# Attention heads whose small matrix products are set side by side on TensorE, in a streaming-encoder block

## The chip, the cores and the metric

One core of one Trainium2 chip runs the whole program. The metric is the device time of one execution in microseconds (us), as the median of several runs. TensorE (PE in the profile; PEld is its weight load), VectorE (DVE), ScalarE (ACT), GpSimd (POOL) and the queue of SyncE (SP) that issues most transfers each run their own list of instructions in order, and wait for each other through semaphores.

## What is computed

One layer over 256 tokens of width 4096, all in float32. A normalized input `xn` is projected to seven parts; 16 attention heads of width 128 and a convolution module run beside each other; their gated outputs are projected back, and a second gated embedding follows.

```python
xn = rms_norm(h, norm_in_g[i])
q, k, v, z_a, a_c, g_c, z_c = split(xn @ w_in[i])           # 4 x 2048, 3 x 2048 columns
y_a = chunked_attention(q, k, v, rel_table[i])              # softmax(q k / sqrt(128) + bias) v
y_a = rms_norm(y_a, attn_out_g[i]) * silu(z_a)
y_c = conv_module(a_c, g_c, w_dw[i], ...)                   # u = a * sigmoid(g); 31 taps; LayerNorm; swish; @ w_pw
y_c = rms_norm(y_c, conv_out_g[i]) * silu(z_c)
h = h + concatenate([y_a, y_c]) @ w_out[i]
h = h + sigmoid(rms_norm(h, g) @ w_ple_gate[i] + b) * (p[i] @ w_ple[i])
return rms_norm(h, final_g)
```

With 256 tokens every query block of 128 rows sees only the keys before it: the first block 128 keys, the second 256. So a head's scores are one 128x128 and one 128x256 product, and its probabilities are three blocks of 128x128.

## The kernel before, in words

**The large products.** Every float32 operand of a large product is split into a high part and a remainder (`wh` and `wl` for weights, L199 to L210), and each product is made of three matmuls, high by high, low by high, high by low, at L420. Here these are called **wide steps**: one matmul that moves 512 columns into a PSUM bank. `mixed_product` (L377) walks the weights two row blocks at a time. A weight block arrives in `wt` (five buffers) by a transfer on SP's queue (L480, L482); ScalarE casts it to `wh` and VectorE subtracts to give `wl` (L204, L205; three buffers each); then TensorE takes 12 wide steps on it. Some pairs of blocks ("sevens") use seven products in place of eight, with helper sums `ua` and `uh`, `ul`, and their helper banks are taken from the same four small PSUM banks (`tmp_ps`, L86) that attention uses.

**The small products.** All of these are plain float32 matmuls into `tmp_ps`, and they are called **narrow passes** here: a transpose is one pass of 128 columns, any other float32 product is two passes for each matmul, which the profile shows as two records. They are:

- the transposes of the gated convolution input in `glu_conv` (L822), eight in each of four calls;
- the transposes of queries and keys in `to_heads` (L943);
- for each head in `attention` (L953): the scores S (L958, L959); after the softmax the three transposes T of the probabilities `s` (L977); ScalarE's copy of them to `pT` (L979); the three weighted sums W over the values (L982 to L984).

**Softmax between S and T.** VectorE scales the scores and adds the bias (L965), takes the negative row maximum (L969); ScalarE takes the exponent with the row sums (L970); VectorE takes the reciprocal (L974). After W, ScalarE scales the result into `y` (L986), which lies over the head's own queries.

**What sets the order.** The code is written stage after stage (L1042 to L1063): `glu_conv`, projections of queries, keys and values, `attention(g)` for one group of four heads, and so on for four groups, called group 0 to 3 here. A scheduler of the framework then merges the stages: it goes through the program with priorities by the order in which it is written, places each instruction on its engine when it expects the inputs to be there, and fills the gaps with wide steps of the next stage. That merged order is fixed when the program is built; on the chip each engine only follows its list. So a head's narrow passes stand scattered among the wide steps of the product that comes next in the code. Work put into the list `later` (the taps of the convolution, L787; the LayerNorm of the convolution, L862 to L913) is handed out between the wide steps too. The LayerNorm's centering (L868), squares (L872) and sums (L876) follow right behind group 2.

Of the kernel before, what the change touches and what calls it, by code (L numbers as in the profile page):

```python
# [16 lines left out]
P = 128  # L17
# [8 lines left out]
def hybrid_block(  # L26
# [23 lines left out]
    nc = tc.nc  # L50
    _, T, D = x.shape
    NH = T // P
# [3 lines left out]
    HD = AW // H  # L56
# [5 lines left out]
    GH = NB // HD  # L62
# [23 lines left out]
    def tmp_psum():  # L86
        return ps_tmp.tile([P, 512], F32, tag="tmp", name="tmp_ps")
# [41 lines left out]
    ident = cpool.tile([P, P], F32, name="ident")  # L129
# [210 lines left out]
    def units(text):  # L340

        return [
            (int(u.rstrip("*+-")), "".join(f for f in "*+" if f in u), "-" in u)
            for u in text.split()
        ]
# [4 lines left out]
    first = units("0 1 3 5 7 9 11 13 15 2* 8 4* 10 6* 12 14")  # L350
# [236 lines left out]
    def scaled_pair(w, col, apart, order, r, fills, homes=(), **kw):  # L587

        t, z = [], []

        def on_helpers(helper):
            for dst, src in zip((t, z), sum_tiles(*homes)):
                dst.extend(src)
            nc.scalar.activation(z[0][0], helper["P1"], AF.Identity, scale=r[:, :1])
            helper_sums(helper, z)
            for h, j in QUARTERS[1:]:
                nc.scalar.activation(z[h][j], z[h][j], AF.Identity, scale=r[:, h : h + 1])

        c = mixed_product(w, col, xT, xS, order, on_helpers, fills=fills, apart=apart, **kw)
        for h, j in QUARTERS:  # L600
            stt(
                z[h][j], c[h][j], r[:, h : h + 1], z[h][j],
                ALU.mult, ALU.subtract if j else ALU.add,
            )
        return t

    def square_sum(dst, src, scale=1.0):
        junk = spool.tile([P, NB], mybir.dt.bfloat16, tag="junk", name="junk", bufs=1)
        to = junk.rearrange("q (g d) -> q g d", d=src.shape[2]) if len(src.shape) == 3 else junk[:, : src.shape[1]]
        return nc.scalar.activation(to, src, AF.Square, scale=scale, accum_out=dst)  # L610
# [191 lines left out]
    def glu_conv(c):  # L802
        if c == 0:
            sg, gate = scaled_pair(
                w_in0, o_a, o_g - o_a, first, r_x, (1,), begin=first_pairs
            )
        else:
            sg, gate = scaled_pair(
                w_in0, o_a + c * NB, o_g - o_a,
                *((early, r_x, early_fills) if c == 1 else (early_seven, r_x, seven_fills)),  # L810
                ahead=more_combinations if c == 2 else None,
            )
        for h in range(NH):
            nc.scalar.activation(gate[:, h, :], gate[:, h, :], AF.Sigmoid)
            tt(sg[:, h, :], sg[:, h, :], gate[:, h, :], ALU.mult)
        uT = spool.tile([P, 4, T], F32, tag="hd", name="uT", bufs=5)
        for pair in range(2):
            pt = tmp_psum()
            for i in range(2):
                for h in range(NH):  # L820
                    b = 2 * pair + i
                    nc.tensor.transpose(  # L822
                        pt[:, i * T + h * P : i * T + (h + 1) * P],
                        sg[:, h, b * P : (b + 1) * P],
                        ident,
                    )
            nc.scalar.copy(
                uT[:, 2 * pair : 2 * pair + 2, :], pt.rearrange("q (i t) -> q i t", t=T)
            )
        cv = act.tile([P, 4, T], F32, tag="act", name="cv")  # L830
        for i in range(4):
            for k in reversed(range(TAPS)):
                later.append(partial(conv_tap, cv, uT, i, 4 * c + i, k))
        conv.append(cv)
# [118 lines left out]
    def attention(g):  # L953
        qT, kT, v, bias = qs[g], ks.pop(g), vs.pop(g), biases.pop(g)
        y = qT.rearrange("q g (h d) -> q h g d", h=NH)
        for hd in range(GH):
            sp = tmp_psum()
            nc.tensor.matmul(sp[:, :P], qT[:, hd, :P], kT[:, hd, :P], start=True, stop=True)  # L958
            nc.tensor.matmul(sp[:, P : P + T], qT[:, hd, P:], kT[:, hd, :], start=True, stop=True)  # L959
            s = spool.tile([P, P + T], F32, tag="s", name="s")  # L960
            nm = spool.tile([P, NH], F32, tag="nm", name="nm")
            den = spool.tile([P, NH], F32, tag="den", name="den")
            for h, (lo, hi) in enumerate(((0, P), (P, P + T))):
                n = hi - lo
                nc.vector.scalar_tensor_tensor(  # L965
                    s[:, lo:hi], sp[:, lo:hi], HD ** -0.5, bias[:, hd, n - 1 :: -1],
                    ALU.mult, ALU.add,
                )
                nc.vector.tensor_reduce(nm[:, h : h + 1], s[:, lo:hi], AX.X, ALU.max, negate=True)  # L969
                nc.scalar.activation(  # L970
                    s[:, lo:hi], s[:, lo:hi], AF.Exp, bias=nm[:, h : h + 1],
                    accum_out=den[:, h : h + 1],
                )
            nc.vector.reciprocal(den, den)  # L974
            pt = tmp_psum()
            for j in range(3):
                nc.tensor.transpose(pt[:, j * P : (j + 1) * P], s[:, j * P : (j + 1) * P], ident)  # L977
            pT = spool.tile([P, 3 * P], F32, tag="pT", name="pT")
            nc.scalar.copy(pT, pt[:, : 3 * P])  # L979
            o = tmp_psum()  # L980
            vc = slice(hd * HD, (hd + 1) * HD)
            nc.tensor.matmul(o[:, :HD], pT[:, :P], v[:, 0, vc], start=True, stop=True)  # L982
            nc.tensor.matmul(o[:, HD : 2 * HD], pT[:, P : 2 * P], v[:, 0, vc], start=True, stop=False)
            nc.tensor.matmul(o[:, HD : 2 * HD], pT[:, 2 * P :], v[:, 1, vc], start=False, stop=True)  # L984
            for h in range(NH):
                nc.scalar.activation(  # L986
                    y[:, h, hd], o[:, h * HD : (h + 1) * HD], AF.Identity, scale=den[:, h : h + 1]
                )
        for h in range(NH):
            square_sum(ssq_a[:, h, g : g + 1], y[:, h])  # L990
        y_a.append(y)
# [48 lines left out]
    n_g = H // GH  # L1040
    assert n_g == CW // NB == 4
    glu_conv(0)  # L1042
    glu_conv(1)
    load_bias(0)
    heads((o_q, 0), (o_k, 0))
    heads((o_v, 0), (o_v, 1))
    attention(0)
    glu_conv(2)
    load_bias(1)
    heads((o_q, 1), (o_k, 1))  # L1050
    attention(1)
    glu_conv(3)
    moved = comb_place(spool, "hd", bufs=5)
# [3 lines left out]
    heads((o_q, 2), (o_k, 2))  # L1057
    heads((o_q, 3), (o_v, 2), order=early_six, fills=six_fills)
    attention(2)
    layer_norm_swish()  # L1060
    load_bias(3)
# [105 lines left out]
    for ys, o_z, r_y in ((y_a, o_za, r_a), (y_c, o_zc, r_c)):  # L1167
        for c0 in range(0, len(ys), 2):
            last = ys is y_c and c0 + 2 == len(ys)
# [9 lines left out]
    pT = []  # L1179
# [160 lines left out]
    def sum_of(h, at):  # L1340
        s = end[:, 0, h : h + 1]
        pin(nc.vector.tensor_reduce(s, ssq_f[:, h, :at], AX.X, ALU.add))
        return s
# [36 lines left out]
    for i, cols in enumerate(halves):  # L1380
        part = ps_acc.tile([P, NB], F32, tag="acc", name="part")
# [7 lines left out]
    s = sum_of(1, n_f + 1)  # L1389
# [35 lines left out]
```

## Time and profile before

| what | value |
|---|---|
| median of three runs | 2025.72 us (2024.74 to 2026.13) |
| the profiled execution's own time | 2025.85 us |
| span of its instructions | 2024.1 us |
| PE busy | 2006.7 us (99%) |
| DVE busy | 1926.9 us (95%) |
| ACT busy | 1257.1 us (62%) |
| mean granted TensorE clock | 0.998 |
| the four attention groups begin at | 356.6, 536.6, 797.7 and 893.8 us |

The profiled execution took 1.75 us longer than its span; that part lies before the first and behind the last instruction. Matmuls overlap in the records (a wide step lasts 391 ns on average and the next begins about 227 ns after it), so a step's price is the distance to the next one and not its own length. The chain of waits gives just these distances: it walks back from the end, and each piece is the time by which its instructions pushed the chain on. "x8" after a piece is the number of matmuls in it.

### The profile page before, as it was taken

The page shows a single profiled execution, that of the slowest core. Times are in us where ns is not written, and L with a number is a line of the kernel's source. Part 1 is how long each engine was busy: PE and PEld are TensorE (multiplying, and loading weights), DVE is VectorE, ACT ScalarE, POOL GpSimd, SP SyncE. Part 2 cuts the span into 40 slices and gives each one's busy share as a digit, 9 for nine tenths or more (in the row PEclk, how much of TensorE's full clock was granted, in tenths as well). Part 3 has the DMA queues.
Part 4 walks back from the last instruction along what each step waited for, and adds up shares of the span by engine and source line. Part 5 has one row for each costly group of instructions (what it writes and reads, how often), then busy time and mean ns, then how long its engine had stood idle before and what let it go on. Part 6 is the DMA issues. An engine that isn't in the chain of part 4 may idle for free.

```text
span 2024.1 us, 26329 instructions
## 1 busy us (share of the span) xinstructions
PE 2006.7 (99%) x9043; PEld 1648.0 (81%) x9043; DVE 1926.9 (95%) x2771; ACT 1257.1 (62%) x1634; POOL 65.3 (3%) x71
## 2 busy tenths in 40 slices
PE   9999999999999999999999999999999999999997
PEld 7888888878888888788888888887888888888876
DVE  7999999899999999888999999999999999999998
ACT  7655555665666556776566676765766766656565
POOL 0000000000000000000000000000000000000000
PEclk9999999999999999999999999999999999999999
DMA  8788878679668877556677786876767766666765
GB/s 290 225 233 241 249 221 250 178 220 257 200 198 257 255 206 235 164 176 205 202 239 215 225 244 209 240 239 204 236 215 230 234 200 200 211 218 206 232 207 180
DMA packets 174193, 447.72 MB, mean 221 GB/s; under 512 B 14302, under 2 KB 17518, under 8 KB 174058
## 3 DMA queue, kind: packets, MB, share of 16 engines
q1 hardware_dynamic: 161952, 417.93, 63.8%
q0 software_dynamic: 11456, 27.27, 7.9%
q8 instruction: 71, 1.16, 0.2%
q10 hardware_dynamic: 650, 0.84, 0.1%
q14 instruction: 64, 0.52, 0.1%
HBM read 441.78 MB, written 4.19 MB: 220 GB/s over the span
## 4 chain that ended last, share of the span: by engine, by line
PE 89%; DVE 6%; issue 2%; DMA 1%; ACT 1%; POOLq 0%; POOL 0%; ACTq 0%; DVEq 0%; SPq 0%
PE acc L420 68%; PE acc_P L420 17%; DVE wl L205 2%; DMA wt<-in_w_in_dram 1%; PE tmp_ps L170 1%; DVE cv L787 1%; PE acc L237 1%; DVE ul L205 1%; PE tmp_ps L959 0%; PE tmp_ps L943 0%; PE tmp_ps L977 0%; ACT uh L204 0%; DVE cv L868 0%; ACT wh L204 0%; PE tmp_ps L982 0%
## 5 line engine op out<-in xcount | busy, mean ns | idle before, releaser
L420 PE MATMUL acc<-wh,big_t 128*128 128x512 f32 x4028 | 1240.3, 391 | 0.9 <-ACT big_t L156 0.4
L204 ACT CAST wh<-wt 128x1024 fp32r<-128x1024 f32 (+1 forms) x716 | 684.3, 965 | 493.8 <-PE acc L420 351.7
L420 PEld LDWEIGHTS acc<-wh,big_t 128*128 128x128 f32 x4028 | 753.3, 188 | 157.1 <-issue 1.3
L205 DVE TENSOR_TENSOR wl<-wt,wh 128x1024 fp32r<-128x1024 f32 (+1 forms) x716 | 788.8, 1113 | 33.0 <-ACT wh L204 27.5
L420 PE MATMUL acc<-wl,big_t 128*128 128x512 f32 x1958 | 756.4, 392 | 0.3 <-DVE wl L205 0.2
L420 PEld LDWEIGHTS acc<-wl,big_t 128*128 128x128 f32 x1958 | 367.2, 188 | 78.1 <-DVE wl L205 2.7
L204 ACT CAST uh<-ua 128x1024 fp32r<-128x1024 f32 x187 | 196.6, 1051 | 103.0 <-DVE ua L519 51.7
L205 DVE TENSOR_TENSOR ul<-ua,uh 128x1024 fp32r<-128x1024 f32 x187 | 228.1, 1220 | 6.9 <-ACT uh L204 4.2
L787 DVE SCALAR_TENSOR_TENSOR cv<-uT,dw,cv 128x255 f32<-128x255 f32 (+23 forms) x480 | 203.6, 463 | 1.1
L420 PE MATMUL acc_P<-uh,big_t 128*128 128x512 f32 x570 | 174.6, 391 | 0.1
L204 ACT CAST uh<-ub 128x1024 fp32r<-128x1024 f32 x99 | 104.2, 1053 | 47.9 <-DVE ub L532 39.2
L420 PEld LDWEIGHTS acc_P<-uh,big_t 128*128 128x128 f32 x570 | 106.0, 188 | 24.5 <-ACT uh L204 3.3
L205 DVE TENSOR_TENSOR ul<-ub,uh 128x1024 fp32r<-128x1024 f32 x99 | 120.8, 1220 | 0.8 <-ACT uh L204 0.5
L420 PE MATMUL acc_P<-ul,big_t 128*128 128x512 f32 x285 | 109.7, 392 | 0.2 <-DVE ul L205 0.2
L420 PE MATMUL acc<-uh,big_t 128*128 128x512 f32 x286 | 88.6, 390 | 0.0
L420 PE MATMUL acc_P<-wh,big_t 128*128 128x512 f32 x286 | 88.3, 389 | 0.0
L518 DVE TENSOR_TENSOR ua<-wt 128x512 f32<-128x512 f32 x112 | 76.9, 686 | 10.0 <-DMA wt<-in_w_in_dram 6.2
L519 DVE TENSOR_TENSOR ua<-wt 128x512 f32<-128x512 f32 x112 | 76.8, 686 | 2.7 <-DMA wt<-in_w_in_dram 1.7
L420 PE MATMUL acc_P<-uh,comb_t 128*128 128x512 f32 x228 | 70.3, 391 | 0.3 <-ACT uh L204 0.2
L532 DVE TENSOR_TENSOR ub<-ub,wt 128x512 f32<-128x512 f32 x99 | 68.1, 688 | 1.4
L531 DVE TENSOR_TENSOR ub<-ua,wt 128x512 f32<-128x512 f32 x99 | 67.8, 685 | 0.0
L420 PEld LDWEIGHTS acc_P<-ul,big_t 128*128 128x128 f32 x285 | 53.3, 188 | 13.9 <-DVE ul L205 3.0
(254 smaller groups left out, 1631.0 us busy)
## 6 DMA issues: line engine op xcount, KB each, us to landing
wt<-in_w_in_dram SPq DMA_DIRECT2D x416, 512.0 KB, 4.7
wt<-in_w_out_dram SPq DMA_DIRECT2D x128, 512.0 KB, 4.5
wt<-in_w_ple_gate_dram SPq DMA_DIRECT2D x128, 512.0 KB, 4.2
wt<-in_w_pw_dram SPq DMA_DIRECT2D x32, 512.0 KB, 4.9
ua<-in_w_in_dram SPq DMA_DIRECT2D x31, 512.0 KB, 4.3
ua<-in_w_in_dram POOLq DMA_DIRECT2D x31, 512.0 KB, 8.8
wt<-in_w_in_dram SPq DMA_DIRECT2D x31, 256.0 KB, 2.8
low<-in_w_in_dram POOLq DMA_DIRECT2D x12, 512.0 KB, 8.2
```

The lines of the kernel that those rows point to most:

```text
L170: nc.tensor.transpose(pt[:, i * T + h * P : i * T + (h + 1) * P], src[:, h, b] if len(src.shape) == 4 else src[:, h, b * P : (b + 1) * P], ...
L204: nc.scalar.copy(wh[:, :kc, :], wt[:, :kc, :]),
L205: nc.vector.tensor_tensor(wl[:, :kc, :], wt[:, :kc, :], wh[:, :kc, :].bitcast(F32), ALU.subtract),
L237: nc.tensor.matmul(acc, a, b[:, k, :], start=kb == 0 and kind == 0, stop=kb == kblocks - 1 and kind == 2,)
L420: nc.tensor.matmul(banks[name], a, b, start=name not in begun, stop=final and ends[name] == n and kind == 2 and not (left and name in "P2 ...
L518: plus(ua[:, 0], w0[:, 0], w0[:, 1])
L519: plus(ua[:, 1], w0[:, 1], w1[:, 1])
L531: plus(ub[:, 0], ua[:, 0], w1[:, 1])
L532: plus(ub[:, 1], ub[:, 0], w1[:, 0])
L787: nc.vector.scalar_tensor_tensor(cv[:, i, PAD - k :], uT[:, i, : T + k - PAD], dw[:, b, k : k + 1], cv[:, i, PAD - k :], ALU.mult, ALU.add,)
```

## The change

Attention is cut into three functions: `scores` (S and the softmax), `turned` (T and its copy) and `weighted` (W and the scaling). They are called in a new order: T of a head, W of the head before it, S of the head after it. A helper, `tensor`, ties each of these matmuls to the one before by a dependency without a semaphore, which binds only the scheduler: the chain keeps T, W, S in that order on TensorE, and since all inputs of W and S are there before those of T, nothing stands between them. The three transposes are taken in the order 1, 2, 0. In `glu_conv` the transposes go through the halves of the tokens in reverse (the later half first).

```diff
@@ glu_conv
         for pair in range(2):
             pt = tmp_psum()
-            for i in range(2):
-                for h in range(NH):
+            for h in reversed(range(NH)):
+                for i in range(2):
                     b = 2 * pair + i
                     nc.tensor.transpose(
@@ attention
         y = qT.rearrange("q g (h d) -> q h g d", h=NH)
-        for hd in range(GH):
+        behind = []
+
+        def tensor(ins):
+
+            if behind:
+                tc.add_manual_dep(
+                    ins.ins, behind[0].ins.name,
+                    mybir.DependencyInfo(mybir.DependencyClass.NoSync, mybir.DependencyReason.DATA),
+                    reason="a head's matrix work in one run",
+                )
+            behind[:] = [ins]
+
+        def scores(hd):
+
             sp = tmp_psum()
...
             nc.vector.reciprocal(den, den)
+            return s, den
+
+        def turned(s):
+
             pt = tmp_psum()
-            for j in range(3):
-                nc.tensor.transpose(pt[:, j * P : (j + 1) * P], s[:, j * P : (j + 1) * P], ident)
+            for j in (1, 2, 0):
+                tensor(
+                    nc.tensor.transpose(pt[:, j * P : (j + 1) * P], s[:, j * P : (j + 1) * P], ident)
+                )
             pT = spool.tile([P, 3 * P], F32, tag="pT", name="pT")
             nc.scalar.copy(pT, pt[:, : 3 * P])
+            return pT
+
+        def weighted(hd, pT, den):
+
...
+        ready, old = scores(0), None
+        for hd in range(GH):
+            s, den = ready
+            pT = turned(s)
+            if old:
+                weighted(*old)
+            old = hd, pT, den
+            if hd + 1 < GH:
+                ready = scores(hd + 1)
+        weighted(*old)
```

In the rows below, `s` are a head's probabilities, `pT` their transposes, `z` the values, `qT` and `kT` queries and keys, and `acc_...` the banks of the large product that runs meanwhile. In the changed program L971 and L973 are S, L997 is T and L1011 is W.

On TensorE, in group 2, this stood around the third head before the change:

```order
L420 MATMUL acc_7214<-wl,big_t 128x512
L977 MATMUL tmp_ps<-ident,s 128x128
L420 MATMUL acc_7213<-wh,big_t 128x512 x2
L977 MATMUL tmp_ps<-ident,s 128x128 x2
L420 MATMUL acc_7213<-wl,big_t 128x512
L420 MATMUL acc_7215<-wh,big_t 128x512 x2
L982 MATMUL tmp_ps<-z,pT 128x128
L983 MATMUL tmp_ps<-z,pT 128x128
L984 MATMUL tmp_ps<-z,pT 128x128
L958 MATMUL tmp_ps<-kT,qT 128x128
L959 MATMUL tmp_ps<-kT,qT 128x256
L420 MATMUL acc_7215<-wl,big_t 128x512
```

And this stands there now:

```order
L420 MATMUL acc_7213<-wh,big_t 128x512 x2
L420 MATMUL acc_7213<-wl,big_t 128x512
L997 MATMUL tmp_ps<-ident,s 128x128 x3
L1011 MATMUL tmp_ps<-z,pT 128x128 x3
L971 MATMUL tmp_ps<-kT,qT 128x128
L973 MATMUL tmp_ps<-kT,qT 128x256
L420 MATMUL acc_7215<-wh,big_t 128x512 x2
```

A head had three separate places among the wide steps (one transpose, two transposes, then its weighted sums with the next scores); now it has one, and the weighted sums in it are those of the head before. Over the four groups there were 52 places with narrow passes and there are 21 now. Between S and the first T stood 8, 7 and 7 wide steps for the later heads of this group, and 16, 12 and 12 stand there now.

At the end of group 2, TensorE has the last head's transposes and sums and then the LayerNorm's mean (L856). Before:

```order
L977 MATMUL tmp_ps<-ident,s 128x128
L420 MATMUL acc_7213<-wh,big_t 128x512 x2
L977 MATMUL tmp_ps<-ident,s 128x128 x2
L420 MATMUL acc_7213<-wl,big_t 128x512
L420 MATMUL acc_7215<-wh,big_t 128x512 x2
L982 MATMUL tmp_ps<-z,pT 128x128
L983 MATMUL tmp_ps<-z,pT 128x128
L984 MATMUL tmp_ps<-z,pT 128x128
L856 MATMUL tmp_ps<-lnsum,mean_w 128x256
```

Now:

```order
L420 MATMUL acc_7213<-wl,big_t 128x512
L997 MATMUL tmp_ps<-ident,s 128x128 x3
L1011 MATMUL tmp_ps<-z,pT 128x128 x6
L856 MATMUL tmp_ps<-lnsum,mean_w 128x256
L420 MATMUL acc_7215<-wh,big_t 128x512 x2
```

The last head's own sums (the latter three of the six) now follow its transposes with only the sums of the head before between them, where three wide steps stood. Groups 0 and 1 end in the same way; in group 3 two wide steps stand between the two sets of sums.

On VectorE, the same place goes from the last head's reciprocal (L974) through the LayerNorm's centering (`cv<-cv,mu`) and sums of squares (`sq<-sq`) to the weight halves `wl` for the next wide steps. Before:

```order
L974 RECIPROCAL den<-den 128x2
L205 TENSOR_TENSOR wl<-wt,wh 128x1024
L868 TENSOR_TENSOR cv<-cv,mu 128x256 x14
L876 TENSOR_TENSOR sq<-sq 128x1024
L868 TENSOR_TENSOR cv<-cv,mu 128x256
L876 TENSOR_TENSOR sq<-sq 128x1024
L868 TENSOR_TENSOR cv<-cv,mu 128x256
L205 TENSOR_TENSOR wl<-wt,wh 128x1024 x2
```

Now:

```order
L989 RECIPROCAL den<-den 128x2
L868 TENSOR_TENSOR cv<-cv,mu 128x256 x9
L205 TENSOR_TENSOR wl<-wt,wh 128x1024
L868 TENSOR_TENSOR cv<-cv,mu 128x256 x2
L876 TENSOR_TENSOR sq<-sq 128x1024
L868 TENSOR_TENSOR cv<-cv,mu 128x256 x5
L876 TENSOR_TENSOR sq<-sq 128x1024
L205 TENSOR_TENSOR wl<-wt,wh 128x1024 x2
```

One `wl` has moved behind nine of the centering operations, which themselves wait for the mean `mu`; the pair of `wl` at the end has the same work ahead of it as before, 16 centerings, two sums and one `wl`.

More of the change, by code (lines that the diff above doesn't have):

```diff
@@ L955, in attention @@
         y = qT.rearrange("q g (h d) -> q h g d", h=NH)
-        for hd in range(GH):
+        behind = []
[8 more added lines that the diff above has]
+        def scores(hd):
             sp = tmp_psum()
-            nc.tensor.matmul(sp[:, :P], qT[:, hd, :P], kT[:, hd, :P], start=True, stop=True)
-            nc.tensor.matmul(sp[:, P : P + T], qT[:, hd, P:], kT[:, hd, :], start=True, stop=True)
+            tensor(nc.tensor.matmul(sp[:, :P], qT[:, hd, :P], kT[:, hd, :P], start=True, stop=True))
+            tensor(
+                nc.tensor.matmul(sp[:, P : P + T], qT[:, hd, P:], kT[:, hd, :], start=True, stop=True)
+            )
             s = spool.tile([P, P + T], F32, tag="s", name="s")
@@ L974, in attention @@
             nc.vector.reciprocal(den, den)
+            return s, den
+        def turned(s):
             pt = tmp_psum()
-            for j in range(3):
-                nc.tensor.transpose(pt[:, j * P : (j + 1) * P], s[:, j * P : (j + 1) * P], ident)
+            for j in (1, 2, 0):
+                tensor(
+                    nc.tensor.transpose(pt[:, j * P : (j + 1) * P], s[:, j * P : (j + 1) * P], ident)
+                )
             pT = spool.tile([P, 3 * P], F32, tag="pT", name="pT")
             nc.scalar.copy(pT, pt[:, : 3 * P])
+            return pT
+        def weighted(hd, pT, den):
             o = tmp_psum()
             vc = slice(hd * HD, (hd + 1) * HD)
-            nc.tensor.matmul(o[:, :HD], pT[:, :P], v[:, 0, vc], start=True, stop=True)
-            nc.tensor.matmul(o[:, HD : 2 * HD], pT[:, P : 2 * P], v[:, 0, vc], start=True, stop=False)
-            nc.tensor.matmul(o[:, HD : 2 * HD], pT[:, 2 * P :], v[:, 1, vc], start=False, stop=True)
+            for h, part, kb, first, last in (
+                (0, 0, 0, True, True), (1, 1, 0, True, False), (1, 2, 1, False, True)
+            ):
+                tensor(
+                    nc.tensor.matmul(
+                        o[:, h * HD : (h + 1) * HD], pT[:, part * P : (part + 1) * P], v[:, kb, vc],
+                        start=first, stop=last,
+                    )
+                )
             for h in range(NH):
```

## The prediction, written blind

> **What bounds the kernel now.** I read the page first: its engine shares, and the shares of the chain that ended last.
>
> ```profile
> PE 2006.7 (99%) x9043; PEld 1648.0 (81%) x9043; DVE 1926.9 (95%) x2771; ACT 1257.1 (62%) x1634; POOL 65.3 (3%) x71
> PE 89%; DVE 6%; issue 2%; DMA 1%; ACT 1%; POOLq 0%; POOL 0%; ACTq 0%; DVEq 0%; SPq 0%
> ```
>
> TensorE is the bound, and no wide step is removed, so only gaps between its instructions can be won. But 6% of the chain runs over VectorE: in some stretches time saved on TensorE is given back there. Next, the waits of the whole kernel, for the two lines that the change groups (total us, times, longest):
>
> ```profile
> PEld tmp_ps L982 <- ACT pT L979: 3.4, 11, 0.3
> PEld tmp_ps L977 <- ACT s L970: 2.7, 9, 0.4
> ```
>
> In 11 of 16 heads W waits for ScalarE's copy `pT`, in 9 the first T waits for the exponent. These are waits of the weight load; what of them reaches the matmuls is seen only in the chain. Here it is in group 0 (start, us, what):
>
> ```profile
> 360.93 0.11 PE tmp_ps L977
> ...
> 361.73 1.15 PE acc L420 x5
> 362.88 0.22 PE tmp_ps L982 x2
> ...
> 366.05 0.25 PE tmp_ps L977
> 366.30 0.47 PE acc L420 x2
> 366.77 0.22 PE tmp_ps L977 x2
> 366.98 0.70 PE acc L420 x3
> 367.68 0.36 PE tmp_ps L982 x2
> ```
>
> A pair of narrow passes pushes the chain on by 0.22 us, a single one without a wait by 0.11 (360.93). W's first pair takes 0.22 with five wide steps after T (362.88), and 0.36 with three (367.68): the wait costs 0.14. The first T takes 0.25 at 366.05: its wait costs 0.14. Other heads:
>
> ```profile
> 552.16 0.30 PE tmp_ps L977
> ...
> 816.45 0.17 PE tmp_ps L977
> ...
> 817.31 0.71 PE acc L420 x3
> ...
> 908.98 0.35 PE tmp_ps L982 x2
> ...
> 914.40 8.43 PE acc L420 x37
> ...
> 937.11 55.21 PE acc L420 x243
> ```
>
> T's wait lies between 0.06 (816.45) and 0.19 (552.16). The longest stretch gives the undisturbed step, 55.21/243 = 0.2272. Two steps between narrow passes take 0.47 and not 0.454, three 0.70 and not 0.682, 37 take 8.43 and not 8.406: a switch between wide and narrow costs about 0.02 for each place, whatever the stretch's length.
>
> **The change part by part.**
>
> *W's wait.* In the new order a whole softmax distance lies between `pT` and its use for every head but a group's last. 11 x 0.14 = 1.54 us. Bounds: 0.13 each (0.35 at 908.98) gives 1.4, the whole weight-load wait 3.4.
>
> *T's wait.* 10 to 17 wide steps now stand between S and T, against 7 to 15. The first head of a group has 14 or 15 before and keeps about that: its T has no wait (360.93). 9 waits at 0.09, the value between 0.06 and 0.14, are 0.83 us. Bounds: 9 x 0.06 = 0.5 and 9 x 0.19 = 1.7.
>
> *Places.* 52 - 21 = 31 fewer at 0.02, that is 0.62; `glu_conv` has four fewer, 0.08. Lower bound 0.01 each (0.35), upper 0.03 (1.05).
>
> *A new wait.* In groups 0 to 2 the last head's W comes behind its own T with only the W of the head before between them, 3 x 0.22 = 0.67. From T's end (366.98) to the end of W's first pair (367.68 + 0.36) it takes 1.06 where TensorE waits; without a wait it would be 0.67 + 0.22 = 0.89. The wait is 0.17, three times: 0.51. All wide steps are queued behind it on TensorE. In group 3 two wide steps (0.47) stand there as well and cover it. Bounds: nothing, and 3 x 0.4, the longest weight-load wait in the rows above.
>
> Gross: 1.54 + 0.83 + 0.70 - 0.51 = 2.56 us, about 0.65 in each group. SyncE's queue changes by a few swapped neighbours, GpSimd's not at all, and the passes are the same in number: nothing is charged for them. `y` of a head is written later, but its readers (the squares of L610) come after the group.
>
> *What is given back.* From group 0 the chain runs on TensorE to this place, and from there into a transfer:
>
> ```profile
> 392.91 1.37 PE acc L420 x6
> ...
> 395.93 8.65 DMA wt<-in_w_in_dram
> ```
>
> TensorE is ahead of it in the chain, so the transfer starts earlier with TensorE; I count group 0's 0.65 as kept, with its loss as a bound. The stretches behind groups 0 and 1 (columns: start and end, length, then PE, PEld, DVE, ACT and POOL busy, clock, DMA share, GB/s):
>
> ```profile
> 400.00:420.00 20.00, 19.79 (x86) 15.78 (x85) 15.62 (x18) 8.93 (x10) 0.00 (x0) 1.00 0.64 203
> 420.00:440.00 20.00, 19.05 (x84) 15.37 (x84) 17.95 (x20) 13.18 (x15) 0.00 (x0) 1.00 0.65 216
> 460.00:540.00 80.00, 80.00 (x362) 65.96 (x361) 79.95 (x135) 43.03 (x51) 4.87 (x4) 1.00 0.85 245
> 540.00:600.00 60.00, 60.00 (x284) 49.18 (x283) 58.97 (x99) 36.73 (x59) 1.22 (x1) 1.00 0.63 190
> 600.00:620.00 20.00, 19.66 (x87) 15.90 (x86) 18.64 (x23) 12.81 (x15) 0.00 (x0) 1.00 0.68 216
> ```
>
> Behind group 0 VectorE has slack (15.62 of 20). Behind group 1 TensorE stalls for 0.34 in the last of these windows, and VectorE, which it waits for there, is busy for all but 0.05 us before the group and all but 1.03 from 540 to 600. What TensorE wins in group 1 it keeps only as far as VectorE can use it, by waiting less. Its longest wait in the group is this one, for the scores:
>
> ```profile
> 555.35 0.62 DVE L965 SCALAR_TENSOR_TENSOR s<-tmp_ps,bias 128x128 f32<-128x128 f32 x2 [0.48 <-PE tmp_ps L959]
> ```
>
> By there TensorE has won two heads' share, some 0.4, and VectorE comes to that wait no earlier than before. So 0.4 of its 0.48 goes; I take 0.4 of 0.65 as kept and **0.25 as given back**. Bounds: nothing, and all 0.65.
>
> At the end of group 2 stands a chain over VectorE (chain of waits, then ScalarE's rows of the same place):
>
> ```profile
> 818.99 0.37 ACT qT L986
> ...
> 819.57 1.23 DVE wl L205
> 820.79 4.70 DVE cv L868 x14
> 825.49 1.14 DVE sq L876
> ...
> 828.43 1.15 DVE wl L205
> 829.62 5.98 PE acc L420 x25
> ```
>
> ```profile
> 820.12 0.38 ACT L851 ACTIVATE mu<-tmp_ps 128x256 f32<-128x256 f32 x1
> 822.04 1.06 ACT L204 CAST wh<-wt 128x1024 fp32r<-128x1024 f32 x1 [0.94 <-PE acc L420]
> 823.00 2.95 ACT L872 ACTIVATE sq<-cv 128x1024 f32<-128x1024 f32 x3
> ```
>
> TensorE waits for `wl` at 829.62, 12.3 us behind the end of the last T (817.31). The mean `mu` was there at 820.12 + 0.38 = 820.50, 3.2 behind T, and VectorE had made a `wl` meanwhile (819.57). Now three wide steps (0.71) are gone from between T and `mu`, and W of the head before (0.67) has come in: I take 3.1. Behind it VectorE has 16 centerings at 4.70/14 = 0.336 (5.37), two sums and two `wl` at 1.14 (4.56): `wl` is done 13.0 behind T. TensorE reaches that step at 0.67 + 0.17 + 0.67 + 0.43 (both W, the wait, the mean) and 47 steps x 0.2272 = 10.68, 12.6 behind T; so a stall of 0.4 stays. T itself ends earlier, by 0.67 (the W that now follows it), by 0.7 (savings up to there), less one step (0.23), so by 1.1. Since `wl` comes 13.0 and no longer 12.3 behind it, TensorE goes on 0.4 earlier and not 0.65: **0.25 to 0.35 given back**, I take 0.35. VectorE goes on pacing behind it.
>
> Behind group 3 TensorE runs without a stall in the chain (914.40 and 937.11 above): its share is kept.
>
> **Sum.** 2.56 - 0.25 - 0.35 = 1.96. The profiled execution took 2025.85 (span 2024.1 and 1.75 around it), 0.13 above the median 2025.72; so 2023.9 for such an execution, **2023.8** as a median. From the bounds of the parts, the forecast's own range is 2022.6 to 2025.0. Less than about 4 us (0.2%) a measurement of this kernel cannot tell from no change, so this is "the same".
>
> **The rivals.**
>
> *Nothing is given back.* VectorE finds room in its 1.03 us and behind the LayerNorm: 2.56 stays, 2023.2; with T's wait at its upper bound 2022.3. For it speaks the 0.48 of wait; against it the 79.95 of 80. Chance 0.13.
>
> *The stalls behind the groups go too.* If VectorE and the transfers get their inputs earlier, TensorE's idle time in 400 to 440 (0.21 + 0.95) and 600 to 620 (0.34) goes with the rest, and the new wait (0.51) stays out: 2.56 + 1.50 + 0.51 = 4.57, 2021.2. Against it: those stalls end behind VectorE and DMA, whose work is unchanged. Chance 0.13, nine tenths of it below 2021.7.
>
> *All is given back but group 3.* If each of groups 0 to 2 runs into its stall at the old time, 0.65 is left: 2025.1. Chance 0.10. Near it lies the case in which the change doesn't do what it says: if a switch costs by the pass and not by the place, 0.70 falls away, 2024.5; that is inside the forecast's range.
>
> *Slower, by the LayerNorm at the end of group 2.* One `wl` moved behind nine centerings, all of which wait for `mu`, and ScalarE's casts and squares alternate there (822.04, 823.00). If the squares come behind casts that they preceded, each one shifts the sums, and the `wl` pair behind them, by 1.05. Two casts cost 2.1 and TensorE stalls that much longer, which VectorE does not give back: 1.96 - 2.1 = -0.14, 2026.0; with a third, 2027.0. It decides from a shift of 1.96 us on; beyond 2029.8 it would take six casts. For it: VectorE's 4.70 in one piece; against: the pair has the same work of VectorE ahead of it as before. Chance 0.08, a tenth of it above 2029.8.
>
> *Slower, by the clock.* TensorE's clock could fall in the longer runs of pure narrow passes, 13 passes each within a group. Its nearest row holds `glu_conv`'s run of transposes:
>
> ```profile
> 1304.00:1309.00 5.00, 5.00 (x32) 4.39 (x31) 3.48 (x5) 3.12 (x8) 0.00 (x0) 1.00 0.60 184
> ```
>
> The granted clock is 1.00 there. If each of 21 runs brought 13 wide steps at half speed, the price would be 21 x 13 x 0.227 = 62 us, 2086. Chance 0.01. The Trainium skill, page "TensorE: Matmul & The Clock Gate", Part 4 (PE-mode transpose), says that full rate "doesn't engage" for transposes in that mode, because they don't count as busy time in the same way; by that rule grouping would cost up to those 62 us, and the row does not bear it out.
>
> **How the numbers follow.** Forecast 0.55, the others 0.13, 0.13, 0.10, 0.08, 0.01. Below 2021.7 lies most of the second rival: faster 0.12. Above 2029.8 lie the clock and a little of the LayerNorm: slower 0.02. The rest is the same: 0.86. The range leaves out half of the second rival, half of the LayerNorm's and the clock's: 2021.4 to 2026.4, some 0.12.
>
> **What would show it.** Right: in the table of waits, W's 11 entries fall to 3 and T's 9 to none; the chain shows W's first pair at 0.22 within a group, and at 0.39 (0.22 + 0.17) for the last head of groups 0 to 2; TensorE's idle time at 829 stays near 0.4 and that of 600 to 620 grows by about 0.25. Wrong: a stall above 1 us behind group 2, a wait for `s` that remains, or TensorE's mean clock below 0.998. The prediction would also be wrong if wide steps next to a run of narrow passes lost more than 0.02.

## The result, and the profile after it

| | time, us | ratio to the kernel before, 95% interval |
|---|---|---|
| before | 2025.95 (22 runs, 2024.62 to 2028.38) | |
| changed | 2028.89 (22 runs, 2027.30 to 2030.82) | 1.0014 (1.0008 to 1.0020) |
| forecast | 2023.8, range 2021.4 to 2026.4 | 0.9990 |

The change made the kernel slower by 2.9 us (1.6 to 4.1 by the interval), and the time lies outside the range. The profiled execution is the longest of the 22 (2030.82 us; span 2029.0 against 2024.1 before), so its profile shows more loss than the median has. Its page (busy time of each engine; shares of the chain that ended last by engine):

```profile
PE 2007.8 (99%) x9043; PEld 1649.6 (81%) x9043; DVE 1926.6 (95%) x2771; ACT 1255.4 (62%) x1634; POOL 65.3 (3%) x71
PE 84%; DVE 9%; issue 3%; DMA 3%; ACT 1%; POOLq 0%; POOL 0%; ACTq 0%; DVEq 0%
```

Every engine has as many instructions as before, and none is busy for more than 1.1 us longer. But the share of VectorE in the chain went from 6% to 9%, that of transfers from 1% to 3%: the new time lies between instructions, where TensorE waits for VectorE and VectorE for a transfer.

What the change was made for did happen. The weight-load waits, in the table of waits of the changed kernel (L997 is T, L1011 is W; total us, times, longest):

```profile
PEld tmp_ps L997 <- ACT s L985: 1.5, 7, 0.3
PEld tmp_ps L1011 <- ACT pT L1000: 0.2, 1, 0.2
```

and the end of group 1 in its chain of waits (start, us, what):

```profile
549.33 0.33 PE tmp_ps L997 x3
549.66 0.67 PE tmp_ps L1011 x6
550.33 0.22 PE tmp_ps L971 x2
...
553.28 0.44 PE tmp_ps L997 x3
553.73 1.50 PE tmp_ps L1011 x12
```

W's 11 waits are one. T still has seven of its nine, but little of them reaches the matmuls: three passes take 0.33 us, three times 0.11, in all but three of the 16 heads (0.44 for the last head shown here, 0.35 for two others). The last head's W waits as forecast: twelve passes take 1.50 and not 1.34, a wait of 0.16 (forecast 0.17).

The loss is behind group 1. Here are the queue of SyncE, GpSimd's queue and VectorE in the timeline of the kernel before (start, us, engine, operation; idle time before it in brackets). A `ua` is a helper block for a seven: SyncE loads its first half (L462), then GpSimd adds the second half by an accumulating transfer (L463). "x3" is the number of transfers or instructions that a row puts together, as far as they lie in the stretch that was asked for.

```profile
565.78 4.34 SPq L482 DMA_DIRECT2D wt<-in_w_in_dram  x2
570.88 0.37 SPq L462 DMA_DIRECT2D ua<-in_w_in_dram  x1
572.51 3.24 SPq L482 DMA_DIRECT2D wt<-in_w_in_dram  x3
576.18 1.22 POOL L463 DMA_DIRECT2D ua<-in_w_in_dram  x1 [54.84 <-DVE ua L531]
580.51 0.69 DVE L518 TENSOR_TENSOR ua<-wt 128x512 f32<-128x512 f32 x1
581.11 0.69 DVE L519 TENSOR_TENSOR ua<-wt 128x512 f32<-128x512 f32 x1
```

The same place in the changed kernel:

```profile
568.37 0.37 SPq L462 DMA_DIRECT2D ua<-in_w_in_dram  x1
569.50 10.51 SPq L482 DMA_DIRECT2D wt<-in_w_in_dram  x5
572.80 1.22 POOL L463 DMA_DIRECT2D ua<-in_w_in_dram  x1 [52.90 <-DVE wl L205]
580.56 0.69 DVE L518 TENSOR_TENSOR ua<-wt 128x512 f32<-128x512 f32 x1 [0.94 <-DMA wt<-in_w_in_dram]
582.16 0.69 DVE L519 TENSOR_TENSOR ua<-wt 128x512 f32<-128x512 f32 x1 [0.92 <-DMA wt<-in_w_in_dram]
```

In the changed program this one `ua` stands ahead of a weight load on SyncE's queue that it followed before (the second of the two that begin at 565.78). So it is issued 2.5 us earlier (568.37, 570.88), and it lands at 572.1 and not at 575.5 (3.8 and 4.6 us behind its issue). GpSimd's transfer, which needs the first half landed, starts 0.7 us behind that landing in both traces, although the bracket names VectorE; it starts 3.4 us earlier now (572.80, 576.18), beside the two weight loads that VectorE needs next. VectorE has no slack there and waits 0.94 and 0.92. How long the loads took that were issued from 571 to 575 us (before: 572 to 576), from the answers on line L482 alone, changed kernel first, then before; two of the three loads have their landing on record in either trace:

```profile
DMA to landing us min/median/max: 5.1/6.4/7.8
```

```profile
DMA to landing us min/median/max: 4.4/4.5/4.5
```

To see where time goes stage by stage, the wide steps of two traces are laid side by side, since all kernels here have the same 8517 matmuls of the large products in the same stages. The table gives by how much TensorE fell behind the first profile of the kernel before within a stretch (us, minus is a gain; from the start of the same-numbered wide step in either trace; the times are those of before):

| trace | group 0, 355 to 380 | group 1 and behind, 517 to 620 | end of group 2, 790 to 841 | group 3, 893 to 915 | behind it, 915 to 1001 | output projection, 1468 to 1505 |
|---|---|---|---|---|---|---|
| before, second trace | +0.04 | +0.37 | -0.02 | -0.01 | -0.08 | -0.58 |
| changed | -0.51 | +1.95 | -0.21 | -0.54 | +0.51 | +2.21 |
| changed, second trace | -0.51 | +2.83 | -0.19 | -0.51 | +0.43 | +0.59 |

In group 0 and in group 3 half a microsecond each is won, in both traces. Behind group 1 two to three are lost, and behind group 3 what was won there is lost again. The last column is not put down to the change: it lost 2.2 in one trace and 0.6 in the other, and 0.73 in a kernel with the attention of before (`glu_only`, below).

### The profile page after: what moved, and what is told of

Same layout as the page of the kernel before. It is cut to its first block, busy times and chain, and to the rows that moved or that the text cites. A ratio compares the mean times of both kernels' runs of the same rounds, so it can differ in the third digit from the quotient of the medians.

```text
span 2029.0 us, 26324 instructions
## 1 busy us (share of the span) xinstructions
PE 2007.8 (99%) x9043; PEld 1649.6 (81%) x9043; DVE 1926.6 (95%) x2771; ACT 1255.4 (62%) x1634; POOL 65.3 (3%) x71
## 4 chain that ended last, share of the span: by engine, by line
PE 84%; DVE 9%; issue 3%; DMA 3%; ACT 1%; POOLq 0%; POOL 0%; ACTq 0%; DVEq 0%
PE acc L420 63%; PE acc_P L420 16%; DVE wl L205 3%; DMA wt<-in_w_in_dram 2%; DVE ul L205 1%; DVE cv L787 1%; PE tmp_ps L170 1%; PE acc L237 1%; DMA wt<-in_w_out_dram 1%; PE tmp_ps L1011 1%; ACT wh L204 0%; PE tmp_ps L973 0%; PE tmp_ps L943 0%; ACT uh L204 0%; PE tmp_ps L997 0%
```

## The experiments

Two theories were held against each other. **Queue theory**: the helper block's new place on SyncE's queue makes the loss. **VectorE theory**: the loss comes at the ends of groups 2 and 3, where VectorE waits for the mean and for ScalarE's squares.

**Second traces.** Both kernels unchanged, `after2` and `before2`.

> The changed kernel as it is, once more, for a second trace. Two theories of where its loss arises are compared. Queue theory: on SyncE's queue the helper block ua of the product behind group 1 now stands ahead of one weight load; GpSimd's accumulating transfer, which waits for it, starts 3.4 us earlier beside two weight loads, each lands about 3.5 us later than before, and VectorE, which has no slack there, waits. It expects the two waits of VectorE for a transfer near 580 us again (0.94 and 0.92 in the first trace) and TensorE behind the kernel before by 1.3 us after step 2550. Rival (VectorE theory): the time is lost at the ends of groups 2 and 3, where VectorE waits for the mean mu (3.3) and for ScalarE's squares (2.2); it expects these two again. What both call scatter, if it is gone: 2.2 us between 1484 and 1510 us, in the output projection, and 0.5 each near 1162 and 1242 us.

> The kernel before as it is, once more, for a second trace, to see how far two executions of one program differ stage by stage. Queue theory: no wait of VectorE for a transfer at 578 to 584 us. Rival: waits of VectorE there come and go by themselves, up to 1 us each, in either kernel.

2029.90 and 2027.18 us (one execution each). The second trace of the changed kernel has the waits near 580 again, 0.43 and 2.59; that of before has none over 0.1 us up to 592. The waits behind groups 2 and 3 are there in the changed kernel's traces as well, but the table shows no more than 0.5 lost there.

**The helper block put back**, `a_ua_back`. With `wt_loads` the list of SyncE's weight loads, a dependency without a semaphore binds the order on the queue. In the trace nothing else stands otherwise on any engine or queue:

```diff
...
+                ua_load = nc.sync.dma_start(ua, columns(col + apart, 0))
+                ua_loads.append(ua_load)
+                if len(ua_loads) == 22:
+                    tc.add_manual_dep(ua_load.ins, wt_loads[-4].ins.name,
+                        mybir.DependencyInfo(mybir.DependencyClass.NoSync, mybir.DependencyReason.DATA), ...)
```

> The changed kernel with one helper block's transfer put back behind the weight load that it had overtaken on SyncE's queue; nothing else stands otherwise on any engine. Queue theory: the two waits near 580 us are gone, 1.8 to 2.3 us come back, about 2026.8, within 1 us of the kernel before. Rival (VectorE theory): no change, 2028.9, ratio to the kernel before 1.0014.

2026.12 us (11 runs), ratio 1.0003 (0.9994 to 1.0011). GpSimd's transfer starts late again:

```profile
576.10 1.22 POOL L472 DMA_DIRECT2D ua<-in_w_in_dram  x1 [55.61 <-DVE cv L798]
...
579.79 0.68 DVE L529 TENSOR_TENSOR ua<-wt 128x512 f32<-128x512 f32 x1
580.39 0.68 DVE L530 TENSOR_TENSOR ua<-wt 128x512 f32<-128x512 f32 x1
```

One pair of transfers exchanged on one queue is worth 2.8 us by the medians, more than the 1.8 to 2.3 expected: the queue theory holds, and the VectorE theory, which expected 2028.9, falls as the cause of the loss.

**The same exchange in the kernel before**, `b_ua_ahead`: the helper block is asked for one pair of blocks earlier (`sums_ahead`), and the weight load is made to follow it. In the trace all else keeps the order of the kernel before.

```diff
+            if len(ua_loads) == 21 and len(wt_loads) == 190:
+                sums_ahead(n + 1)
...
+            if len(wt_loads) == 192:
+                tc.add_manual_dep(
+                    wt_loads[190].ins, ua_loads[21].ins.name,
+                    mybir.DependencyInfo(mybir.DependencyClass.NoSync, mybir.DependencyReason.DATA),
...
```

> The kernel before with that same transfer put ahead of that same weight load, nothing else. Queue theory: VectorE waits near 580 us, 1.5 to 2.3 us slower than before, about 2027.9, ratio 1.0007 to 1.0011. Rival (VectorE theory): 2026.0, ratio 1.0000.

2028.20 us (11 runs), ratio 1.0012 (1.0003 to 1.0021): as expected in size. But the way there is another one, as its timeline and waits show:

```profile
571.56 0.37 SPq L464 DMA_DIRECT2D ua<-in_w_in_dram  x1
571.98 4.43 SPq L488 DMA_DIRECT2D wt<-in_w_in_dram  x4
...
576.17 1.22 POOL L465 DMA_DIRECT2D ua<-in_w_in_dram  x1 [54.70 <-DVE wl L205]
```

```profile
DVE ua L531 <- DMA wt<-in_w_in_dram: 2.5, 1, 2.5
```

GpSimd starts no earlier than before. Here SyncE stands at the helper block for 5.0 us, since its buffer comes free only at 571.5; the weight load behind it goes out at 571.98 and not at 569.75, and four loads leave within 4.4 us. The last of them, for which VectorE waits, is issued at 576.0, next to GpSimd's transfer (576.17), where in the kernel before it was 0.8 us ahead. So this run has the later, closer loads and again a load beside GpSimd's transfer; it doesn't part the two, and it doesn't tell which one acts in the changed kernel, where the helper block's buffer came free earlier (it was issued at 568.37).

**Only GpSimd's transfer held back**, `a_pool_late` and `a_pool_late2`. The helper block stays ahead, as in the changed kernel; its second half waits for a sum of VectorE:

```diff
...
+                if len(added) == 22:
+                    tc.add_manual_dep(added[-1].ins, pluses[-2].ins.name,
+                        mybir.DependencyInfo(mybir.DependencyClass.Sync, mybir.DependencyReason.DATA), ...)
```

> The changed kernel with the helper block's first half still ahead of the weight load on SyncE's queue, but with GpSimd's accumulating transfer of that block made to wait for VectorE's sum of an earlier pair, so that it starts near 576 us as in the kernel before and not at 572.8. Nothing stands otherwise in any engine's order. If it is GpSimd's transfer beside the two weight loads that costs the time: both loads land within 4.6 us of their issue, VectorE has no wait near 580, about 2026.6. If it is the helper block's first half itself that pushes the weight loads back: no change, 2028.9.

2028.78 us (11 runs), ratio 1.0014 (1.0005 to 1.0023). The trial failed as a test: that sum was an earlier one, already done, and the transfer started as early as in the changed kernel. It serves as one more run of the changed kernel, with the added dependency in the program:

```profile
572.22 1.22 POOL L465 DMA_DIRECT2D ua<-in_w_in_dram  x1 [52.76 <-DVE wl L205]
...
583.05 0.69 DVE L527 TENSOR_TENSOR ua<-wt 128x512 f32<-128x512 f32 x1 [3.30 <-DMA wt<-in_w_in_dram]
```

With `pluses[-1]` in place of `pluses[-2]`:

> The wait that took no effect in the last trial, put on the next sum: the changed kernel, with the helper block's first half ahead of the weight load as it stands there, and GpSimd's accumulating transfer made to wait for VectorE's sum near 575 us, so that it starts near 576 and not at 572.2. If it is GpSimd's earlier transfer that slows the two weight loads: they land within 5.5 us of their issue, TensorE loses at most 1.3 us between steps 2440 and 2560 and not 2.3 to 2.6, and the time is about 2027.3. If the place on SyncE's queue itself is the cause: 2.3 to 2.6 again, 2028.8.

2025.19 us (11 runs), ratio 1.0000 (0.9991 to 1.0009). Now the transfer starts at 575.49, VectorE doesn't wait for these loads, and TensorE loses 0.24 between steps 2440 and 2560 (592 to 620 us), less than expected:

```profile
575.49 1.22 POOL L465 DMA_DIRECT2D ua<-in_w_in_dram  x1 [56.69 <-DVE cv L795]
...
578.41 0.69 DVE L526 TENSOR_TENSOR ua<-wt 128x512 f32<-128x512 f32 x1
579.02 0.68 DVE L527 TENSOR_TENSOR ua<-wt 128x512 f32<-128x512 f32 x1
```

In the traces the order on every engine and queue is the same in the changed kernel, in `a_pool_late` and in `a_pool_late2`; only the start of this transfer differs, and the loss is gone. So it is GpSimd's transfer beside the two weight loads that slows them, and not the first half ahead of them.

**The two parts of the change**, `att_only` (the transposes in `glu_conv` as before) and `glu_only` (attention as before).

> The attention part of the change alone; the gated transposes stand as before. The helper block overtakes the weight load in this program too. Queue theory: 2028 to 2029, as the whole change, and the waits near 580 us. Rival (the gated transposes in one run make the loss, by way of VectorE's taps): 2026.2 or less.

> The gated transposes in one run alone; attention stands as before, and the helper block stays behind the weight load. Queue theory: 2026.2, within 0.4 of the kernel before (four places fewer, 0.08). Rival: 2028 to 2029.

2028.81 (1.0013, 1.0004 to 1.0022) and 2026.61 (1.0003, 0.9994 to 1.0012), 11 runs each. The loss belongs to attention's new order, whose program has the exchange on the queue; the transposes' program hasn't.

**What is given back behind groups 2 and 3.** Three kernels start from `a_ua_back`. An empty place is an entry of the list `later` that hands out no work (`rest`). `a_mu` moves four of the LayerNorm's empty places; `a_ra_late` moves one statement behind the convolution's product; `a_ra_mu` does the latter and adds four places without taking any away.

```diff
         later.append(lambda: mean(st["s"]))
-        later.extend(rest)
+        later.extend(2 * rest)
...
         later.append(lambda: variance(st["q"]))
-        later.extend(rest)
+        later.extend(rest[:2])
         later.append(lambda: spread(st["s"]))
-        later.extend(rest)
+        later.extend(rest[:2])
```

```diff
     attention(3)
-    r_a = rstd_of(ssq_a, AW, "r_a")
...
+    r_a = rstd_of(ssq_a, AW, "r_a")
     r_c = rstd_of(ssq_c, CW, "r_c")
```

> The changed kernel with the helper block back behind the weight load, and two waits of VectorE eased: the row sum r_a, for which VectorE stands 2.2 us behind group 3, is taken behind seven later instructions of VectorE, and four more empty places lie between the LayerNorm's mean and its centering, which puts two centerings fewer ahead of a wl. Theory that VectorE gives the gain back behind groups 2 and 3: the two stalls of TensorE near 943 and 995 us (0.26 and 0.27) fall below 0.1 each and the stall near 829 below 0.3, 0.6 to 0.9 better than with the helper block alone, about 2025.4. Rival (the gain was never there, or is lost elsewhere): 2026.1, and TensorE behind the kernel before by no less at step 4140.

2036.48 us (5 runs), 1.0053 (1.0040 to 1.0066): 10 us slower, 8.1 of it in group 3 and behind it (steps 3700 to 4140). Since everything in the list `later` is handed out four places later, the LayerNorm's splitting (`big_t`, L924) now stands in VectorE's list between a head's maximum (`nm`) and what follows, in the chain at the begin of group 3:

```profile
896.42 0.52 DVE nm L995 x2
896.94 1.34 DVE big_t L924 x4
...
900.15 1.15 DVE wl L205
901.30 0.04 issue
901.34 0.79 PE acc L422
```

TensorE waits for a `wl` that comes behind all this. The next two have the same number of places as `a_ua_back` and are not slow.

> The changed kernel with the helper block back behind the weight load, and four of the LayerNorm's empty places moved from behind the variance to between the mean and the centering; the number of places is the same. The wl that stood behind nine centerings now stands behind six. Theory that the end of group 2 gives the gain back: TensorE gains 0.8 to 1.2 us between steps 3372 and 3480 (0.25 with the helper block alone), about 2025.3. Rival: what is won there is lost again behind it, 2026.1.

2024.53 us (11 runs), 0.9994 (0.9985 to 1.0003).

> The changed kernel with the helper block back behind the weight load, and the row sum r_a, for which VectorE stands 2.2 us behind group 3, taken some seven instructions later on VectorE; the work is the same. Theory that VectorE gives group 3's gain back: TensorE's two stalls near 943 and 995 us (0.26 and 0.27) fall, and of the 0.54 gained between steps 3700 and 3760 at least 0.4 is left at step 4140 (0.02 with the helper block alone); 2025.7. Rival (the stalls come from work that is in neither kernel's attention): 0.0 left, 2026.1.

2025.43 us (11 runs), 0.9998 (0.9989 to 1.0007). The times can't be told from `a_ua_back`; the stretches can:

| trace | group 0 | group 1 and behind | end of group 2 | group 3 | behind it | output projection |
|---|---|---|---|---|---|---|
| `b_ua_ahead` | +0.02 | +2.39 | 0.00 | +0.01 | -0.14 | -0.06 |
| `att_only` | -0.51 | +2.47 | -0.16 | -0.53 | +0.18 | +0.45 |
| `glu_only` | +0.01 | +1.60 | -0.03 | -0.01 | -0.11 | +0.73 |
| `a_ua_back` | -0.51 | +0.09 | -0.19 | -0.54 | +0.56 | +1.11 |
| `a_pool_late2` | -0.50 | -0.14 | -0.21 | -0.51 | +0.43 | +0.06 |
| `a_ra_late` | -0.52 | -0.04 | -0.23 | -0.53 | +0.24 | +0.76 |
| `a_mu` | -0.47 | -0.35 | -0.52 | -0.45 | -0.03 | +0.45 |
| `best` (below) | -0.49 | -0.45 | -0.51 | -0.44 | +0.02 | +0.57 |

The traces of `b_ua_ahead`, `glu_only` and `a_ua_back` are of the longest of their eleven executions, so these rows show more loss than their medians have.

At the end of group 2 `a_mu` gains 0.52 where the others gain about 0.2; between steps 3372 and 3480 it is 0.62, less than the 0.8 to 1.2 expected. Its chain holds no VectorE there, only TensorE's 81 wide steps in a row at 0.2272:

```profile
815.70 0.43 PE tmp_ps L867 x2
816.13 18.40 PE acc L422 x81
```

Of group 3's gain `a_ra_late` keeps 0.53 - 0.24 = 0.29, not the 0.4 expected. The wait of 2.2 us only moved to the next VectorE instruction behind ScalarE's squares. `a_mu` keeps nearly all of it; that its VectorE comes to those places earlier is argued and not shown. One trace speaks against too tidy a reading: `glu_only` lost 1.6 in and behind group 1 without the exchange, with waits of VectorE for loads near 580 (0.29 and 0.55). Landings there scatter; it is the medians that separate the kernels (2028.2 to 2028.9 with the exchange and its wait, 2024.5 to 2026.6 in the other programs but `a_ra_mu`).

**Both cures in one kernel**, `best`: `a_pool_late2` with the places of `a_mu`.

> Both cures that worked, in one program: the changed order with the helper block ahead of the weight load, GpSimd's transfer held back to VectorE's sum near 575 us, and four empty places moved to between the LayerNorm's mean and its centering. If the two causes are separate, their gains add up: against the changed kernel -3.7 (GpSimd's transfer) and about -1.0 (the end of group 2), 2024.2 and below, clear of the kernel before (ratio 0.9990). Rival (VectorE gives all back in the end, so that only stalls move): 2025.2 to 2026, not to be told from the kernel before.

2025.25 us (11 runs), 0.9999 (0.9990 to 1.0008). That is the rival's time; the gains did not add up to one that can be measured. In the stretches they are there: between 355 and 1001 us TensorE gains 2.6 in this trace and 2.5 in that of `a_mu`, against 0.6 in the second trace of before. Why the medians show no more of it is open. No version here is shown to beat the kernel before; the best median is that of `a_mu`, and its interval holds 1.

## Why the prediction was wrong, point by point

- **The step that failed** is the sentence on the queues: "SyncE's queue changes by a few swapped neighbours, GpSimd's not at all, and the passes are the same in number: nothing is charged for them." One of those swaps was `ua` ahead of `wt`, and although GpSimd's list is the same, its transfer waits for what SyncE loaded, so it moved by 3.4 us. TensorE lost 2.3 to 2.5 us at that place (steps 2440 to 2560) in both traces of the changed kernel, more than the 1.96 forecast as gain; its idle time from 600 to 620 us, forecast to grow by 0.25, grew from 0.34 to 1.80. The exchange was in plain sight in the order; what it needed was the question which other queue waits for the moved transfer, and what is in flight there. None of the rivals had a transfer as its cause.
- **The gain** isn't there in full without that loss either: `a_ua_back` and `a_pool_late2` have the new order and the late transfer, and their ratios are 1.0003 and 1.0000, with intervals that begin at 0.9994 and 0.9991, just above the 0.9990 forecast. The points below say what became of its parts.
- **W's and T's waits**: W's went as forecast in the main, and the new wait was 0.16 for 0.17; in group 3, where two wide steps were to cover it, W's last six passes still took 0.76 and not 0.67. T's waits were forecast to go to none, and seven remain, which the prediction names as a sign of being wrong; in the chain they cost 0.15 in all. Group 0 gained 0.51 where about 0.65 was forecast, group 3 0.51 to 0.54. The terms of the sum were a fifth too large.
- **Group 0**: whether its 0.51 is kept can't be told. Between 405 and 436 us the second trace of before gains 0.9 by itself.
- **Group 1**: forecast 0.4 kept. In the six traces with the new order and no early transfer, 0.36 to 0.43 are won from 517 to 606 us (steps 2150 to 2500), as forecast. At the next stop, where TensorE waits for `uh` behind VectorE's sums (608 to 611 us), they lose between nothing and 0.5, and the second trace of before loses 0.44 there by itself. So what is left of the 0.4 behind it cannot be told from the scatter.
- **End of group 2**: forecast 0.3 kept, measured 0.2. The working of the chain held: 0.57 are won up to step 3430 (829 us), and 0.37 are given back at `wl`, for 0.35 forecast. In the chain of the changed kernel:

```profile
817.41 0.33 PE tmp_ps L997 x3
...
820.52 0.28 ACT mu L851
...
829.68 1.15 DVE wl L205
830.83 0.04 issue
830.88 0.73 PE acc L420 x2
```

T ends at 817.74, `mu` is there 3.1 later and `wl` 13.1 later (forecast 3.1 and 13.0). The rival of a late LayerNorm did not come about.
- **Group 3**: "its share is kept" was wrong. It was earned (0.54) and lost again (0.51) behind it, most of it in two places (near 944 and 995 us). The first, in the chain of the changed kernel:

```profile
943.87 0.46 issue
944.33 0.69 DVE y_c L1152
945.02 0.04 issue
945.07 0.96 PE acc L420 x3
```

and the busy time in the stretch around it, changed and then before (columns as in the prediction: TensorE is the first behind the length):

```profile
940.00:950.00 10.00, 9.90 (x44) 7.87 (x44) 9.57 (x14) 7.52 (x14) 0.00 (x0) 1.00 0.41 143
```

```profile
940.00:950.00 10.00, 10.00 (x46) 8.08 (x45) 9.93 (x16) 8.38 (x14) 0.00 (x0) 1.00 0.52 184
```

The chain of before showed TensorE alone there, and the forecast took that for slack of VectorE. A chain shows who came last, not by how much. The weight loads of TensorE at this place show it, before and then changed:

```profile
944.16 0.30 PEld L420 LDWEIGHTS acc<-wh,big_t 128*128 128x128 f32 x2 [0.23 <-DVE y_c L1110]
```

```profile
945.06 0.30 PEld L420 LDWEIGHTS acc<-wh,big_t 128*128 128x128 f32 x2 [0.52 <-DVE y_c L1152]
```

One already waited 0.23 for VectorE's `y_c` before, hidden behind the matmuls still running. It waits 0.29 longer now, about what TensorE loses there (0.26).
- **The clock** stayed: a mean of 0.998 in both kernels, and 1.00 from 536 to 560 and from 797 to 820 us, where 13 narrow passes stand in a row. The row at 1304 us, which the prediction takes for `glu_conv`'s transposes, holds 16 transposes of the attention's output in a row (L170, 1.9 us). The rule of the Trainium skill weighed in the prediction (page "TensorE: Matmul & The Clock Gate", Part 4, PE-mode transpose) doesn't show in these runs of passes, which have wide steps on both sides; no run here has more than 16 transposes in a row.
- **The chances**: 0.86 stood for "the same" (2021.7 to 2029.8). The median lies in it, but the measurement was sharper than the 0.2% used, and its interval is clear of no change. The way to a slower kernel that the prediction named, by the LayerNorm, was not this one.

Why the scheduler put `ua` ahead in the new order was not looked into, and the scatter of the output projection (-0.6 to +2.2) is not explained.

## What to carry to other kernels

When a change reorders one engine, read the transfer queues in the new order line by line, and for each exchanged pair ask which other queue waits for it and which loads are then in flight; here one exchange outweighed all that was won on TensorE. Before counting a gain as kept, look for the next place where another engine delivers just in time, since a chain with one engine alone doesn't show how close the others are. Where the bounding engine alternates with a second one, small gains on it may only be lent: here group 3's half microsecond was gone 80 us later.

## What the runs showed of the hardware

Beside GpSimd's accumulating transfer a 512 KB weight load took up to 7.8 us from issue to landing in the changed kernel, and not 4.5 as before. Over all traces: where GpSimd's transfer started 0.1 to 0.3 us behind the load that VectorE needs first at this place, that load took 7.0 to 7.9 us (changed, its second trace, `att_only`, `a_pool_late`); 6.7 where it started 1.9 us behind (`b_ua_ahead`); 4.3 to 6.1 where it started 2.5 to 4.0 us behind, but 7.1 in `glu_only`. So the landings scatter all the same, and an early start of GpSimd is not the only way to a late one. The Trainium skill, page "DMA: Bandwidth & Descriptors", section "SWDGE vs HWDGE vs iDMA", says that GpSimd's and SyncE's transfers feed different queues inside each DMA engine, and that the engine goes round between them. The traces fit this, since a load already issued slows down when GpSimd's transfer joins it; the queues inside an engine are not seen in any run here.
